# Down's left sums made on VectorE in gate and up, squares a product ahead, and a last stage that starts with the second token half

## The chip, the cores and the metric

The kernel runs on one core of a Trainium2 chip, in one launch. The metric is the device time of one execution in microseconds (us); the times below are of three runs, and the median counts. Times in the trace come from one further, profiled execution.

## The reference, cut to what matters

One layer of a decoder block, batch 1, 1024 tokens, width 1024, all in float32:

```
x1  = x + merge(dilated_attention(n), hgrn2(n))       # n = rmsnorm(x)
h   = silu(rmsnorm(x1) @ w_gate) * (rmsnorm(x1) @ w_up)     # hidden width 2816
x2  = x1 + h @ w_down
g   = sigmoid(rmsnorm(x2) @ w_pg)                     # 1024 x 1024
out = rmsnorm(x2 + g * (p @ w_pe))                    # p: 1024 tokens x 256
```

The change touches the feed-forward part (gate, up, down) and the last stage (w_pg, w_pe, the final norm).

## The kernel before, in words

Activations lie transposed: a tile is 128 channels by 512 or 1024 tokens; `halves` are the token halves c0 and c1 of 512. Each float32 product is three matmuls: an operand is split into a rounded part `hi` (a cast on ACT) and the rest `lo` (a subtraction on DVE), and TensorE adds hi·hi, hi·lo and lo·hi into one PSUM bank (L275, L276, L277 in `product_part`; L192 to L194 in `gemm`).

Gate and up, and then down, use a 2x2 Winograd form: seven block products instead of eight, with sums of blocks as operands. In gate and up the loop over `ft` makes 22 units, each seven products of 12 matmuls. A unit's weights are loaded raw into `w0` and `w1`; four sums s1 to s4 are made from them on POOL (L292 to L295); for each product one left operand `q` is split (L299 on ACT, L300 on DVE). `q` has a ring of five slots, so the splits run up to five products ahead of TensorE. Each unit's result `us` and further sums `t` of it are stored to DRAM, where down finds its right operands (`first_dram`, `second_dram`, `t_dram`).

Down computes products in the order 1, 5, 2, 6, 3, 7, 4. Each has four row tiles d = 0 to 3, and each tile three parts of 4, 4 and 3 blocks: 4 x 33 = 132 matmuls to a product. Per part, `down_lefts` loads one or two raw blocks of w_down into a ring of three slots (256 KB for four blocks, 192 KB for three); products 5, 6, 3 and 7 need a sum on DVE (L1019, L1021, L1023, L1025), and then the split follows (L1027 on ACT, L1028 on DVE) into the same ring of five `q`. Right blocks `B` of the next product are loaded into a staging tile `st` and split (L235 on ACT, L236 on DVE), three after each tile's result (`ahead`). Results are read out of PSUM by `down_result`: copies `m57` on ACT after product 5, and additions and multiplications on DVE after the others. Rows 0 to 3 of x2 are complete (both halves) after product 3, rows 4 to 7 get their second half in product 7 and their first in product 4.

After product 4's tiles, `next_norm` scales x2 by the norm's gain and splits it (L221 on ACT, L222 on DVE) and adds its square to `sums` (L946 on ACT, the addition L947 on POOL). The last stage `ple` then multiplies by w_pg (`weight` splits it: L171 on POOL, L172 on DVE) and by w_pe (p is split by L216 and L217), first half first; a product with ones (L209) adds the squares over the channels.

All DMAs that matter here are issued from SP's queue, which is in order, as is every engine. The order on each engine is decided at build time by a scheduler that follows data, ring slots and the order of the code.

Of the kernel before, what the change touches and what calls it, by code (L numbers as in the profile page):

```python
# [12 lines left out]
F32 = mybir.dt.float32  # L13
# [116 lines left out]
def block_kernel(ctx: ExitStack, tc: tile.TileContext, a: dict, out: bass.AP):  # L130
# [148 lines left out]
    def winograd(units, qr, sr, after=()):  # L279
# [3 lines left out]
        def lefts():  # L283

            for src0, src1, n in units:
# [6 lines left out]
                pool.tensor_add(s1, a21, a22)  # L292
                pool.tensor_sub(s3, a11, a21)
# [65 lines left out]
    act.activation(scratch, eps, AF.Square)  # L359
# [637 lines left out]

    S_SLOTS = [ring([i]) for i in range(16, 22)]

    def down_lefts():  # L1000

        need = {1: ((0, 0),), 5: ((1, 0), (1, 1)), 2: ((0, 1),), 6: ((0, 0),), 3: ((0, 1),), 7: ((0, 0), (1, 0)), 4: ((1, 1),)}
        sums = {}
        for j in DOWN_ORDER:
            for d in range(4):
                for p, (k0, n) in enumerate(PARTS):
                    raw = RAW.next([P, 2, n, P], F32, "w")
                    for i, (row, half) in enumerate(need[j]):
                        nc.sync.dma_start(raw[:, i], a[f"w_dn{p}"][d + 4 * row, half])
                    x, src = raw[:, 0], raw[:, 0]  # L1010
                    if j == 5:
                        if p == 0:
                            sums[d, 0] = S_SLOTS[d].next([P, 2, n, P], F32, "s")
                        if p == 2 and d % 2 == 0:
                            sums[d, 2] = S_SLOTS[4 + d // 2].next([P, 2, n, P], F32, "s")
                    if j in (5, 6, 3):
                        src = sums[d - d % 2, 2][:, d % 2] if p == 2 else sums[d, 0][:, p]
                        if j == 5:
# [14 lines left out]
        [(a["w_gu"][2 * ft], a["w_gu"][2 * ft + 1], 4) for ft in range(NF)], QR, ring([47, 48]), down_lefts()  # L1033
# [17 lines left out]
    rs, down_right = None, {n: [] for n in range(len(DOWN_ORDER))}  # L1051
    for ft in range(NF):
# [19 lines left out]
        us = T.next([P, S], F32, "us")  # L1072
        if ft >= NH:
# [30 lines left out]
    XA, KEEP, OUT = ring([29, 30, 31, 34, 16, 17, 18, 19]), [ring([22, 23]), ring([24, 25])], ring([8, 48])  # L1104
    xa, sums, x3 = {}, pair(SUMS, "sums"), {}
    SQ2 = ring([47])
    X3 = ring(RS[7] + RS[2] + [13, 14, 15, 20, 21, 24, 25, 26])

# [16 lines left out]
    def next_norm(i, c):  # L1125
# [5 lines left out]
        square(i, c, x, sums, SQ2, pool)  # L1131

    def down_result(j, d, b):
# [4 lines left out]
        if j == 2:  # L1138
            t = OUT.next([P, 512], F32, "t")
            x = residual(d)  # L1140
# [4 lines left out]
        if j == 3:  # L1145
            t = OUT.next([P, 512], F32, "t")
# [203 lines left out]
```

## Time and profile before

| | us |
|---|---|
| three runs | 1670.85, 1673.15, 1665.83 (median 1670.85) |
| the profiled execution: time, span of its trace | 1667.34, 1665.5 |
| TensorE busy (x7968 matmuls), mean granted clock | 1604.8, 0.987 |
| VectorE busy | 1117.4 |
| ScalarE busy | 649.5 |
| GpSimd busy | 559.9 |

Busy times are sums over the span and overlap between engines. The engines are called PE (TensorE), DVE (VectorE), ACT (ScalarE), POOL (GpSimd) and SP. PE is busy nearly all the time, so what a change can bring lies in the stretches where it is not; the rows below show them.

### The profile page before, as it was taken

Reading aid. Unit: us, or ns where it says so; the run is one execution under the profiler, and the core shown is the slowest. Engines: PE = TensorE matmul, PEld = TensorE weight load, DVE = VectorE, ACT = ScalarE, POOL = GpSimd, SP = SyncE. Lnnn points to the kernel's source line nnn. Section 1 sums busy time; section 2 is a strip of 40 time slices with the busy share of each in tenths; the row PEclk is TensorE's granted clock in tenths of the full one; section 3 lists DMA queues with packets and bytes.
Section 4 is the critical chain, followed back from the end, with each engine's and each line's share of the span. In section 5 each row is a group of like instructions: output and inputs, shape, how many; then the busy total and the mean of one; then the engine's idle time right before and its main releaser. Section 6 shows DMA issues by size and latency. Waiting matters only on the chain.

```text
span 1665.5 us, 21614 instructions
## 1 busy us (share of the span) xinstructions
PE 1604.8 (96%) x7968; PEld 1332.7 (80%) x7968; DVE 1117.4 (67%) x1673; ACT 649.5 (39%) x1128; POOL 559.9 (34%) x413
## 2 busy tenths in 40 slices
PE   9899998999999999999999999999999999998996
PEld 7687787898998888888887888888888778775786
DVE  8955664678665566765557666666777668798536
ACT  6523332467552011532345333333333554444334
POOL 2555652223322111114354343444554000034214
PEclk9999998999999999999999999999999999999998
DMA  5232343332124322533432323334444887654202
GB/s 197 76 115 102 139 157 116 96 90 72 52 92 146 109 102 77 196 133 114 153 113 83 113 90 99 111 114 140 152 140 163 276 292 232 233 154 128 63 1 101
DMA packets 84778, 213.54 MB, mean 128 GB/s; under 512 B 9408, under 2 KB 16320, under 8 KB 84672
## 3 DMA queue, kind: packets, MB, share of 16 engines
q1 hardware_dynamic: 84528, 212.14, 39.0%
q8 instruction: 62, 1.02, 0.3%
q14 instruction: 44, 0.36, 0.1%
q10 hardware_dynamic: 144, 0.02, 0.0%
HBM read 155.51 MB, written 56.62 MB: 127 GB/s over the span
## 4 chain that ended last, share of the span: by engine, by line
PE 47%; DVE 7%; DMA 4%; issue 2%; ACT 2%; POOL 1%; DVEq 0%; SPq 0%; POOLq 0%; ACTq 0%
PE u L275 8%; PE u L276 8%; PE u L277 8%; PE mm L194 5%; PE mm L192 5%; PE mm L193 5%; DVE B L236 2%; PE g L666 1%; DMA w<-w_dn 1%; DVE q L1028 1%; PE dnb L277 1%; PE dnb L275 1%; PE dnb L276 1%; DMA st<-t_dram 1%; DMA st<-first_dram 1%
## 5 line engine op out<-in xcount | busy, mean ns | idle before, releaser
L275 PE MATMUL u<-B,q 128*128 128x512 f32 x776 | 303.8, 394 | 5.6 <-ACT m L333 3.6
L276 PE MATMUL u<-B,q 128*128 128x512 f32 x776 | 304.4, 392 | 3.7 <-DVE B L236 3.7
L277 PE MATMUL u<-B,q 128*128 128x512 f32 x776 | 303.4, 391 | 1.9 <-DVE q L300 1.9
L275 PEld LDWEIGHTS u<-B,q 128*128 128x128 f32 x776 | 146.6, 189 | 41.5 <-ACT m L333 8.2
L276 PEld LDWEIGHTS u<-B,q 128*128 128x128 f32 x776 | 146.7, 189 | 35.4 <-DVE B L236 5.2
L277 PEld LDWEIGHTS u<-B,q 128*128 128x128 f32 x776 | 146.6, 189 | 32.9 <-DVE q L300 2.3
L299 ACT CAST q<-s 128x512 fp32r<-128x512 f32 x128 | 79.5, 622 | 157.6 <-PE u L277 145.6
L300 DVE TENSOR_TENSOR q<-s,q 128x512 fp32r<-128x512 f32 x128 | 107.5, 842 | 49.2 <-ACT q L299 48.1
L192 PE MATMUL mm<-xh,wh 128*128 128x512 f32 (+1 forms) x352 | 138.1, 392 | 0.1
L194 PE MATMUL mm<-xh,wl 128*128 128x512 f32 (+1 forms) x352 | 132.0, 375 | 1.8 <-DVE wl L172 1.7
L193 PE MATMUL mm<-xl,wh 128*128 128x512 f32 (+1 forms) x352 | 131.4, 373 | 0.0
L171 POOL TENSOR_SCALAR wh<-wr 128x1024 fp32r<-128x1024 f32 (+1 forms) x55 | 57.3, 1044 | 203.9 <-PE mm L193 100.1
L300 DVE TENSOR_TENSOR q<-w,q 128x512 fp32r<-128x512 f32 x96 | 85.0, 886 | 60.2 <-ACT q L299 60.0
L193 PE MATMUL mm<-l,wh 128*128 128x512 f32 (+1 forms) x296 | 115.0, 389 | 1.3 <-DVE l L910 0.9
L192 PE MATMUL mm<-h,wh 128*128 128x512 f32 (+1 forms) x296 | 114.7, 389 | 0.9 <-POOL wh L171 0.8
L194 PE MATMUL mm<-h,wl 128*128 128x512 f32 (+1 forms) x296 | 114.0, 386 | 1.0 <-DVE wl L172 1.0
L299 ACT CAST q<-w 128x512 fp32r<-128x512 f32 x96 | 59.7, 622 | 121.8 <-PE u L277 69.1
L544 POOL TENSOR_SCALAR p<-p,rd 128x128 f32<-128x128 f32 (+3 forms) x64 | 53.1, 831 | 144.3 <-DVE rd L543 126.4
L1082 POOL TENSOR_TENSOR us<-v 128x512 f32<-128x512 f32 x22 | 38.7, 1757 | 155.0 <-DVE v L337 142.2
L194 PEld LDWEIGHTS mm<-xh,wl 128*128 128x128 f32 x352 | 66.3, 188 | 14.5 <-DVE wl L172 3.1
L484 PE MATMUL mm<-wh,xh 128*128 128x256 f32 x256 | 76.4, 300 | 0.0
L485 PE MATMUL mm<-wl,xh 128*128 128x256 f32 x256 | 73.7, 288 | 0.8 <-DVE wl L172 0.8
(303 smaller groups left out, 3847.6 us busy)
## 6 DMA issues: line engine op xcount, KB each, us to landing
w<-w_gu SPq DMA_DIRECT2D x44, 512.0 KB, 3.9
w<-w_dn SPq DMA_DIRECT2D x72, 256.0 KB, 3.9
t_dram<-t SPq DMA_DIRECT2D x44, 256.0 KB, 4.3
w<-w_in SPq DMA_DIRECT2D x20, 512.0 KB, 3.8
st<-t_dram SPq DMA_DIRECT2D x20, 512.0 KB, 4.5
w<-w_dn SPq DMA_DIRECT2D x36, 192.0 KB, 3.8
wr<-w_in SPq DMA_DIRECT2D x13, 512.0 KB, 3.7
sg_dram<-gt SPq DMA_DIRECT2D x24, 256.0 KB, 2.0
```

What stands on the lines that cost most here:

```text
L171: pool.tensor_scalar(hi, raw, 1.0, 0.0, ALU.mult, ALU.add)
L192: pe.matmul(dst, hi[:, k, :], xh[:, c0 : c0 + n], start=first and k == ks[0], stop=False)
L193: pe.matmul(dst, hi[:, k, :], xl[:, c0 : c0 + n], start=False, stop=False)
L194: pe.matmul(dst, lo[:, k, :], xh[:, c0 : c0 + n], start=False, stop=last and k == ks[-1])
L275: pe.matmul(dst, q[:, 0, k], bh, start=first and not more and k == 0, stop=False, skip_group_check=more)
L276: pe.matmul(dst, q[:, 0, k], bl, start=False, stop=False, skip_group_check=more)
L277: pe.matmul(dst, q[:, 1, k], bh, start=False, stop=end, skip_group_check=more)
L299: act.copy(q[:, 0], left[m])
L300: dve.tensor_sub(q[:, 1], left[m], f32(q)[:, 0])
L484: pe.matmul(b, xh[:, ts_], hi[:, k % 4, :], start=(k == 0), stop=False)
L485: pe.matmul(b, xh[:, ts_], lo[:, k % 4, :], start=False, stop=False)
L544: pool.tensor_scalar(pr[:, :n], pr[:, :n], rd, 0.0, ALU.mult, ALU.add)
```

## The change

It has six parts. In gate and up, s1 and s3 are made on DVE (`eng`), s2 and s4 stay on POOL. Twenty-four sums that down's products 5 and 7 need are made in gate and up by `down_sums`: two loads, a sum on DVE (L1010), a store to `left_dram`. Down's products 5 and 7 then load one finished block where they loaded two and added; product 6, which found product 5's sum in SBUF, loads it again and so loads two blocks where it loaded one. The casts of the right blocks are put behind the casts of `q` on ACT (`issue_after`). In down's results, product 7 no longer multiplies `u` and adds it on POOL; product 4 adds `u` first and multiplies after. The squares of rows 0 to 3 are made by product 7, their six additions on POOL; those of rows 4 to 7 are added on DVE. The last stage starts with c1, has the first w_pg weight split during product 4, and finds slots for its weights that are free by then.

```diff
-                pool.tensor_add(s1, a21, a22)
-                pool.tensor_sub(s3, a11, a21)
+                eng.tensor_add(s1, a21, a22)
+                eng.tensor_sub(s3, a11, a21)
...
+    left_dram = {j: [dr.tile([4, P, n, P], F32, name=f"s{j}_{p}_dram") for p, (_, n) in enumerate(PARTS)] for j in (5, 7)}
+    LS = ring([28, 32])
+
+    def down_sums():
+        for d in range(4):
+            for p, (_, n) in enumerate(PARTS):
+                for j in (5, 7):
+                    raw = LS.next([P, 2, n, P], F32, "ls")
+                    other = (d + 4, 1) if j == 5 else (d, 0)
+                    nc.sync.dma_start(raw[:, 0], a[f"w_dn{p}"][other])
+                    nc.sync.dma_start(raw[:, 1], a[f"w_dn{p}"][d + 4, 0])
+                    (dve.tensor_add if j == 5 else dve.tensor_sub)(raw[:, 0], raw[:, 0], raw[:, 1])
+                    nc.sync.dma_start(left_dram[j][p][d], raw[:, 0])
+                    yield
...
-                    for i, (row, half) in enumerate(need[j]):
-                        nc.sync.dma_start(raw[:, i], a[f"w_dn{p}"][d + 4 * row, half])
+                    if j in need:
+                        row, half = need[j]
+                        nc.sync.dma_start(x, a[f"w_dn{p}"][d + 4 * row, half])
+                    else:
+                        nc.sync.dma_start(x, left_dram[j][p][d])
+                    if j == 6:
+
+                        nc.sync.dma_start(raw[:, 1], left_dram[5][p][d])
...
-                        if j == 5:
-                            dve.tensor_add(src, x, raw[:, 1])
-                        elif j == 6:
-                            dve.tensor_sub(src, src, x)
+                        if j == 6:
+                            dve.tensor_sub(src, raw[:, 1], x)
...
-                    if j == 7:
-                        dve.tensor_sub(src, x, raw[:, 1])
...
+        if 0 < ft < NF - 2:
+            for _ in islice(to_sum, 1 + (ft % 3 == 0)):
+                pass
...
-        square(i, c, x, sums, SQ2, pool)
+
+    def add_square(i, c, eng):
+        x = xa[i][:, halves[c]]
+        if i == 0:
+            act.activation(sums[c], x, AF.Square)
+        else:
+            turn["sq"] += 1
+            sq = squares[:, turn["sq"] % 2]
+            act.activation(sq, x, AF.Square)
+            eng.tensor_add(sums[c], sums[c], sq)
...
-            dve.tensor_mul(u[d], u[d], rs[0])
-            pool.tensor_add(x[:, c0], x[:, c0], u[d])
         if j == 4:
-            t, x = OUT.next([P, 512], F32, "t"), xa[d + 4]
-            dve.tensor_mul(t, b, rs[0])
+            t, x = temp(), xa[d + 4]
+            dve.tensor_add(t, b, u[d])
+            dve.tensor_mul(t, t, rs[0])
             dve.tensor_add(x[:, c0], x[:, c0], t)
...
-            for _ in islice(ahead, 3):
-                pass
-
+
+            with tc.issue_after(latest(act_engine)):
+                for _ in islice(ahead, 3):
+                    pass
+
+            if j == 7:
+                for c in range(2):
+                    add_square(d, c, pool)
             if j == 4:
-                for c in range(2):
-                    next_norm(d, c)
+                if d == 1:
+                    w_pg0 = weight(a["w_pg"][0], [P, KD, P], WH, WL)
+                next_norm(d, 1)
                 next_norm(d + 4, 1)
+                add_square(d + 4, 1, dve)
+                next_norm(d, 0)
     for d in range(4):
         next_norm(d + 4, 0)
+        add_square(d + 4, 0, dve)
...
     for d in range(4):
-        w = weight(a["w_pg"][d], [P, KD, P], WH, WL)
-        for cs in halves:
+        w = weight(a["w_pg"][d], [P, KD, P], WH, WL) if d else w_pg0
+        for cs in halves[::-1]:
             ple(d, w, cs.start, 512)
```

On DVE, in an early unit of gate and up, before (L300 is the `lo` of a left, L335 and L337 and L1063 read PSUM):

```order
L1089 TENSOR_TENSOR t1_1007_7710<-us_1006_7702 128x512
L300 TENSOR_TENSOR q_1015_7751<-s12_994_7615,q_1015_7751 128x512
L335 TENSOR_TENSOR v_1012_7718<-u_1010_7716,m_1011_7717 128x512
L300 TENSOR_TENSOR q_1020_7777<-w0_1016_7767,q_1020_7777 128x512
L1063 TENSOR_TENSOR gs_1021_7792<-u_1008_7714,rs_1000_7682 128x512
L300 TENSOR_TENSOR q_1022_7795<-s12_1018_7771,q_1022_7795 128x512
L300 TENSOR_TENSOR q_1023_7810<-s34_1019_7772,q_1023_7810 128x512
L300 TENSOR_TENSOR q_1024_7825<-w0_1016_7767,q_1024_7825 128x512
L337 TENSOR_TENSOR v_1012_7718<-u_1009_7715,m_1011_7717 128x512
```

and the same place after (L1010 is a sum for down, `ls` its two-slot tile):

```order
L1010 TENSOR_TENSOR ls_1089_8287<-ls_1089_8287 128x384
L300 TENSOR_TENSOR q_1015_7757<-s12_994_7621,q_1015_7757 128x512
L1010 TENSOR_TENSOR ls_1109_8431<-ls_1109_8431 128x384
L292 TENSOR_TENSOR s12_1018_7777<-w1_1017_7774 128x512
L335 TENSOR_TENSOR v_1012_7724<-u_1010_7722,m_1011_7723 128x512
L300 TENSOR_TENSOR q_1020_7783<-w0_1016_7773,q_1020_7783 128x512
L1081 TENSOR_TENSOR gs_1021_7798<-u_1008_7720,rs_1000_7688 128x512
L300 TENSOR_TENSOR q_1022_7801<-s12_1018_7777,q_1022_7801 128x512
L300 TENSOR_TENSOR q_1023_7816<-s34_1019_7778,q_1023_7816 128x512
L1010 TENSOR_TENSOR ls_1130_8576<-ls_1130_8576 128x512
L1010 TENSOR_TENSOR ls_1131_8581<-ls_1131_8581 128x512
L300 TENSOR_TENSOR q_1024_7831<-w0_1016_7773,q_1024_7831 128x512
```

Two pairs of the sums stand in this unit's row, and so in each of the first six units that have any: the code asks for one or two a unit, the scheduler brings them forward. The sum s1 (L292) stands between them.

On ACT, at the end of product 5, before (`q_1535` is product 2's first left, `B` the right blocks, `m57` the copy that frees a bank):

```order
L1027 CAST q_1533_11199<-s_1521_11130 128x384
L235 CAST B_1537_11231<-st_1536_11229 128x512
L235 CAST B_1538_11234<-st_1536_11229 128x512
L1027 CAST q_1535_11216<-w_1534_11214 128x512
L235 CAST B_1540_11239<-st_1539_11237 128x512
L235 CAST B_1547_11291<-st_1539_11237 128x512
L1137 COPY m57_1461_10779<-dnsp1505_11036 128x512
```

and after:

```order
L1044 CAST q_1551_11280<-w_1550_11278 128x512
L1044 CAST q_1553_11297<-w_1552_11295 128x384
L1044 CAST q_1555_11314<-w_1554_11312 128x512
L1173 COPY m57_1487_10907<-dnsp1528_11153 128x512
L235 CAST B_1557_11329<-st_1556_11327 128x512
L235 CAST B_1558_11332<-st_1556_11327 128x512
```

No right block stands any more between product 5's last left and product 2's first, nor directly ahead of the copy `m57`.

On PE, behind the last matmul of down, before (`sums` with ones, then p with w_pe, with w_pg's c0 half further on):

```order
L277 MATMUL dnov1684_12089<-B_1733_12376,q_1763_12534 128x512
L209 MATMUL mm_1807_12723<-sums_1457_10775,ones_70 128x512
L192 MATMUL mm_1808_12730<-h_1785_12657,wh_1791_12669 128x512
L192 MATMUL mm_1811_12769<-h_1785_12657,wh_1791_12669 128x512
L193 MATMUL mm_1808_12730<-l_1786_12658,wh_1791_12669 128x512
L193 MATMUL mm_1811_12769<-l_1786_12658,wh_1791_12669 128x512
L194 MATMUL mm_1808_12730<-h_1785_12657,wl_1792_12670 128x512
L194 MATMUL mm_1811_12769<-h_1785_12657,wl_1792_12670 128x512
L209 MATMUL mm_1806_12716<-sums_1456_10774,ones_70 128x512
```

and after:

```order
L277 MATMUL dnov1702_12189<-B_1747_12458,q_1774_12616 128x512
L209 MATMUL mm_1799_12771<-sums_1481_10901,ones_70 128x512
L192 MATMUL mm_1797_12745<-xh_1754_12516,wh_1765_12581 128x512
L193 MATMUL mm_1797_12745<-xl_1755_12517,wh_1765_12581 128x512
L194 MATMUL mm_1797_12745<-xh_1754_12516,wl_1766_12582 128x512
L192 MATMUL mm_1797_12745<-xh_1767_12585,wh_1765_12581 128x512
```

What follows down's last matmul is now a whole product of 24 matmuls of c1 with w_pg's first tile, whose operands are all split before down ends; the six of p with w_pe and the second ones-product come behind it. The bank of that product is the one that down's last tile (`dnov`) leaves.

## Rows read from the trace of the kernel before

**Rows 1.** The page's busy time, share of the span and instructions by engine.

```profile
PE 1604.8 (96%) x7968; PEld 1332.7 (80%) x7968; DVE 1117.4 (67%) x1673; ACT 649.5 (39%) x1128; POOL 559.9 (34%) x413
```

**Rows 2.** Windows of 25 us: PE, PEld, DVE, ACT, POOL busy (x instructions), granted clock, DMA share, GB/s.

```profile
1350.00:1375.00 25.00, 22.07 (x88) 17.22 (x88) 15.71 (x26) 14.00 (x26) 0.00 (x0) 0.93 0.84 283
...
1450.00:1475.00 25.00, 24.24 (x106) 19.23 (x105) 20.67 (x34) 12.54 (x22) 2.04 (x2) 1.00 0.77 240
1475.00:1500.00 25.00, 23.20 (x99) 17.93 (x97) 24.94 (x28) 13.58 (x24) 13.61 (x9) 1.00 0.31 86
1500.00:1525.00 25.00, 20.81 (x89) 16.27 (x89) 23.80 (x30) 8.65 (x17) 10.12 (x6) 1.00 0.37 103
1525.00:1550.00 25.00, 20.33 (x71) 13.00 (x70) 18.41 (x18) 9.69 (x12) 10.48 (x8) 0.93 0.52 166
1550.00:1575.00 25.00, 25.00 (x112) 20.71 (x111) 12.69 (x18) 9.83 (x15) 5.75 (x5) 1.00 0.14 43
```

**Rows 3.** Timeline of PE where product 5 ends: start, us, line [idle before <- releaser].

```profile
1355.04 0.39 PE L277 MATMUL dnsp<-B,q 128*128 128x512 f32 x1
1357.35 0.50 PE L275 MATMUL dnb<-B,q 128*128 128x512 f32 x1 [1.92 <-ACT q L1027]
...
1359.82 0.80 PE L275 MATMUL dnsp<-B,q 128*128 128x512 f32 x1 [0.84 <-ACT m L1137]
```

**Rows 4.** Timeline of ACT in the same place.

```profile
1355.64 1.14 ACT L235 CAST B<-st 128x512 fp32r<-128x512 f32 x2 [0.96 <-DMA st<-second_dram]
1356.68 0.61 ACT L1027 CAST q<-w 128x512 fp32r<-128x512 f32 x1
```

**Rows 5.** Windows of product 5 and of product 6.

```profile
1325.00:1357.00 32.00, 30.43 (x135) 24.86 (x133) 23.77 (x41) 16.80 (x32) 0.00 (x0) 1.00 0.91 302
...
1390.00:1421.00 31.00, 31.00 (x138) 25.66 (x138) 27.09 (x47) 13.35 (x24) 0.00 (x0) 1.00 0.73 233
```

**Rows 6.** Groups of instructions from 1450 to 1530 us: busy, mean ns | idle before.

```profile
L947 POOL TENSOR_TENSOR sums<-sums,sq 128x512 f32<-128x512 f32 x13 | 20.3, 1559 | 18.3 <-ACT sq L946 18.3
...
L1157 POOL TENSOR_TENSOR xa<-xa,u 128x512 f32<-128x512 f32 x4 | 7.0, 1738 | 169.0 <-DVE u L1156 159.8 <-issue 6.2 <-PE dnov L277 3.0
...
L1156 DVE TENSOR_TENSOR u<-u,rs 128x512 f32<-128x512 f32 x4 | 2.7, 681 | 0.0
...
L1025 DVE TENSOR_TENSOR w<-w 128x384 f32<-128x384 f32 x3 | 1.6, 550 | 1.0 <-DMA w<-w_dn 1.0
```

**Rows 7.** Timeline of DVE in product 7, and a row of product 4.

```profile
1477.21 0.68 DVE L1025 TENSOR_TENSOR w<-w 128x512 f32<-128x512 f32 x1
...
1478.41 1.77 DVE L236 TENSOR_TENSOR B<-st,B 128x512 fp32r<-128x512 f32 x1
...
1505.51 0.74 DVE L222 SCALAR_TENSOR_TENSOR xl<-xa,vec,xh 128x512 fp32r<-128x512 f32 x1
```

**Rows 8.** Timeline of PE where the last stage begins.

```profile
1528.62 0.73 PE L192 MATMUL mm<-h,wh 128*128 128x512 f32 x2 [0.39 <-POOL wh L171]
1529.69 0.73 PE L193 MATMUL mm<-l,wh 128*128 128x512 f32 x2 [0.34 <-DVE l L217]
1531.43 0.73 PE L194 MATMUL mm<-h,wl 128*128 128x512 f32 x2 [1.01 <-DVE wl L172]
1533.21 1.49 PE L209 MATMUL mm<-sums,ones 128*128 128x512 f32 x2 [1.05 <-POOL sums L947]
```

**Rows 9.** Timeline of DVE there: down's last result and a weight's `lo`.

```profile
1527.41 0.69 DVE L1160 TENSOR_TENSOR t<-dnov,rs 128x512 f32<-128x512 f32 x1 [1.00 <-PE dnov L277]
...
1530.16 1.21 DVE L172 TENSOR_TENSOR wl<-wr,wh 128x1024 fp32r<-128x1024 f32 x1
```

**Rows 10.** Ten units of gate and up (905 to 1095 us), groups of instructions.

```profile
L1083 DVE TENSOR_TENSOR us<-us,gs 128x512 f32<-128x512 f32 x10 | 17.9, 1786 | 0.0
L293 POOL TENSOR_TENSOR s<-w,w 128x512 f32<-128x512 f32 x10 | 17.8, 1776 | 0.5 <-DMA w<-w_gu 0.2
```

**Rows 11.** One line of gate and up by itself: durations, first and last start.

```profile
L1082 POOL TENSOR_TENSOR us<-v x11: 1799/1803/1807, 900.2 to 1090.6; 128x512 f32<-128x512 f32 x11
```

**Rows 12.** A window in gate and up.

```profile
900.00:925.00 25.00, 25.00 (x112) 20.57 (x111) 18.79 (x26) 9.39 (x17) 11.00 (x7) 1.00 0.39 119
```

**Rows 13.** DMA issues of the whole span: KB each, median us to landing.

```profile
w<-w_dn SPq DMA_DIRECT2D x72, 256.0 KB, 3.9
t_dram<-t SPq DMA_DIRECT2D x44, 256.0 KB, 4.3
```

More of the change, by code (lines that the diff above doesn't have):

```diff
@@ L277, in product_part, with winograd @@
             pe.matmul(dst, q[:, 1, k], bh, start=False, stop=end, skip_group_check=more)
-    def winograd(units, qr, sr, after=()):
+    def winograd(units, qr, sr, after=(), eng=pool):
         def lefts():
@@ L358, in block_kernel @@
     scratch = cp.tile([P, 1], F32, name="scratch")
-    act.activation(scratch, eps, AF.Square)
+    act_engine = act.activation(scratch, eps, AF.Square).ins.engine
     warm = MS.next([P, 512], F32, "warm")
@@ L1032, in block_kernel @@
     ffn_unit, next_left, _ = winograd(
-        [(a["w_gu"][2 * ft], a["w_gu"][2 * ft + 1], 4) for ft in range(NF)], QR, ring([47, 48]), down_lefts()
+        [(a["w_gu"][2 * ft], a["w_gu"][2 * ft + 1], 4) for ft in range(NF)], QR, ring([47, 48]), down_lefts(), dve
     )
@@ L1051, in block_kernel @@
     rs, down_right = None, {n: [] for n in range(len(DOWN_ORDER))}
+    to_sum = down_sums()
     for ft in range(NF):
@@ L1100, in block_kernel, with temp @@
             nc.sync.dma_start(t_dram[7][i], t23[:, 1])
-    XA, KEEP, OUT = ring([29, 30, 31, 34, 16, 17, 18, 19]), [ring([22, 23]), ring([24, 25])], ring([8, 48])
+    XA, KEEP, OUT = ring([29, 30, 31, 34, 16, 17, 18, 19]), [ring([22, 23]), ring([24, 25])], ring([8])
     xa, sums, x3 = {}, pair(SUMS, "sums"), {}
-    SQ2 = ring([47])
     X3 = ring(RS[7] + RS[2] + [13, 14, 15, 20, 21, 24, 25, 26])
+    temps, squares = OUT.next([P, 2, 512], F32, "t"), ring([47]).next([P, 2, 512], F32, "sq")
+    turn = {"t": 0, "sq": 0}
+    def temp():
+        turn["t"] += 1
+        return temps[:, turn["t"] % 2]
     def bank_set(n):
@@ L1138, in down_result @@
         if j == 2:
-            t = OUT.next([P, 512], F32, "t")
-            x = residual(d)
+            t, x = temp(), residual(d)
             dve.tensor_mul(t, b, rs[0])
@@ L1145, in down_result @@
         if j == 3:
-            t = OUT.next([P, 512], F32, "t")
+            t = temp()
             dve.tensor_add(t, b, u[d])
@@ L1150, in down_result @@
         if j == 7:
-            t, x = OUT.next([P, 512], F32, "t"), residual(d + 4)
+            t, x = temp(), residual(d + 4)
             dve.tensor_add(m57[d], b, m57[d])
@@ L1194, in block_kernel @@
     wpe = [weight(a["w_pe"][j], [P, 2, 512], PW, PW) for j in range(2)]
-    rs = None
+    rs = {}
     sumf, rf = RF.next([P, S], F32, "sumf"), RF.next([P, S], F32, "rf")
     def ple(d, w, c0, n):
-        nonlocal rs
-        cs = slice(c0, c0 + n)
+        cs, c = slice(c0, c0 + n), c0 // 512
         b = mm()[:, :n]
         gemm(b, w, x3, c0, n, range(KD))
-        if rs is None:
-            rs = pair(RS2, "rs3")
-            token_scale(rs, sums, [T4.next([P, 512], F32, "t") for _ in range(2)])
+        if c not in rs:
+            rs[c] = RS2.next([P, 512], F32, "rs3")
+            rstd_rep(rs[c], sums[c], mm(), 1.0 / D, *(T4.next([P, 512], F32, "t") for _ in range(2)))
         hi, lo = wpe[d // 4]
@@ L1211, in ple @@
         t = T4.next([P, 512], F32, "t")[:, :n]
-        dve.tensor_mul(t, b, rs[c0 // 512][:, c0 % 512 : c0 % 512 + n])
+        dve.tensor_mul(t, b, rs[c][:, c0 % 512 : c0 % 512 + n])
         act.activation(t, t, AF.Sigmoid)
```

17 lines of the change are left out of this document (8 added, 9 removed).

## The prediction

> **What bounds the kernel now.** I read the page's busy times first. PE is busy for 96% of the span [rows 1], so only idle or slow PE time can be won, and the question is where it lies. The windows of 25 us answer that. At its full rate PE does 112 matmuls in 25 us, 0.223 us each (the last of [rows 2]); every matmul that a window lacks is 0.223 us lost, whether PE waited or ran at a lower clock. The window from 1350 lacks 24 matmuls (5.4 us), that from 1450 lacks 6 (1.3), from 1475 13 (2.9), from 1500 23 (5.1) and from 1525 41, which is 9.2, of which I count 1.1 as the slower products with ones and keep 8.1. Together 22.8 us in five windows, all in down and at the change to the last stage. Gate and up show full windows like [rows 12]: nothing can be won there, only lost.
>
> Then the timelines, for each of these places. Where product 5 ends, PE waits 1.92 us for a left and 0.84 us for the copy `m57` [rows 3]. On ACT that left stood behind two casts of right blocks, and those had waited for their transfer [rows 4]: the cause is a late DMA, passed on by ACT's order. The window holds a clock of 0.93 as well [rows 2], between the two levels of 1.2 and 2.4 GHz, after PE had idled; so the loss of 5.4 us is larger than the waits. In product 5 the DMA engines were busy 0.91 of the time at 302 GB/s, in product 6 0.73 at 233 [rows 5]. From 1475 to 1525 the DMA share is only 0.31 and 0.37, but DVE is busy 24.94 and 23.80 of 25 us [rows 2]: DVE is the bound of products 7 and 4. Part of that is not its own work. The same kind of addition takes 0.68 us when alone and 1.77 us when POOL works beside it [rows 7], and POOL has 15 instructions in these 50 us [rows 2]. At the change to the last stage PE waits in turn for `wh`, `l`, `wl` and POOL's last `sums` [rows 8], which are all made only when down has ended.
>
> **The change, part by part.**
>
> Product 5. Twelve parts now load one block instead of two: 8 x 256 KB and 4 x 192 KB, 2.8 MB less of the 9.7 MB that 302 GB/s moved in 32 us, so about 215 GB/s, below what product 6 moves today without a wait [rows 5]. The twelve sums leave DVE, and ACT has the left and the copy ahead of the right blocks. Either alone should remove the waits of [rows 3]. Of 5.4 us I leave 0.5: **-4.9** (bounds 0 and -5.4).
>
> Product 6. It loads what product 5 saved: 7.2 + 2.8 MB in 31 us, 323 GB/s, more than product 5's 302. That is a rate at which the kernel stalled, but here with product 2's lighter stretch ahead of it, in which the three raw slots and five lefts fill, and with the lefts first on ACT. Bounds 0 and +5.4 (product 5's loss again); nearer the lower because of that lead: **+2.0**.
>
> Products 7 and 4. Of DVE's 48.7 us in the 50 from 1475, three `u` multiplications (0.68 each) and two or so sums of product 7's lefts (0.55 to 0.68 [rows 6, 7]) go: 3.2 us. All of POOL's additions go too (L947 1.56 us each, L1157 1.74 [rows 6]; rows 0 to 3 have their six additions earlier). They stretched DVE's work by up to 15 x 1.09 = 16.4 us; I take 13, because POOL's additions did not always meet a DVE instruction of that kind. Added are seven additions of squares, three additions of `u` (0.68 each) and one `wl` of 1.21 us [rows 9]: 8.0. Demand after: 48.7 - 3.2 - 13 + 8.0 = 40.5 us. PE's work in these 50 us is 50 - 8.0 = 42 us. So DVE would still be busy for 96% of it, which is bare cover: the queue is in order, and its instructions come in bunches behind each result. Of the 8.0 us lost I leave 3.0: **-5.0** (bounds 0, if the 13 were only 11 and bunching ate the rest, and -8.0). The 1.3 us of the window from 1450 stay.
>
> The Trainium skill (SBUF — State Buffer, section "Who interferes with whom") says that a VectorE instruction with two inputs in SBUF and a GpSimd instruction that reads SBUF exclude each other, the later one being blocked fully. The trace agrees: 0.68 and 1.77 us in [rows 7]. Taken to the letter, the whole 16.4 us would go and the term would be the full -8.0.
>
> The change to the last stage. Of the 8.1 us, the waits in [rows 8] make 2.8, the rest is low clock behind them and waits further on. Afterwards PE has 24 matmuls of c1 at once (5.4 us), whose operands and whose `wl` exist before down ends, and `l` and the second `sums` are wanted behind these. What is late next is the bank: the first product takes the one that down's last tile leaves, and DVE reads it about 1.0 us after the last matmul and for 0.69 us [rows 9], with one or two instructions of 1.2 us ahead of it in its row. So I leave 3.0: **-5.1** (bounds -2 and -8.1).
>
> Gate and up. s1 and s3 come to DVE (2 x 0.68) where POOL took 1.78 us for s3 [rows 10]. In six units four sums are added (4 x 0.68): 4.1 us in a unit of 19.04 us (190.4 us over ten, [rows 11]). DVE was busy 18.79 of 25 us there, 14.3 in a unit [rows 12], hence 18.4 of 19.04 at worst: it still fits, with five lefts of lead as cover. If that cover goes, each microsecond over is lost. At the very first unit the sum s3 stands before right blocks on DVE. I take **+1.1** for both (bounds 0 and the first rival).
>
> Nothing in the reordering of the token halves changes the number of matmuls.
>
> Sum: -4.9 + 2.0 - 5.0 - 5.1 + 1.1 = -11.9 us against the profiled execution's 1667.3, so 1655.4. The median of the runs shown, 1670.85, lies 3.5 above that execution and the fastest 1.5 below it; I add half of 3.5 and forecast **1657 us**.
>
> **The rivals.**
>
> First, and on the other side: the round trip of down's sums blocks DVE. A pair of sums needs its loads (3.9 us), two additions (1.4) and stores (4.3) [rows 13] before the two slots are free: 9.6 us, and a unit has two such pairs, 19.2 us of a unit of 19.04. The additions stand in DVE's row ahead of lefts and results, so a late load stops all that PE needs. For six units at 9.6 us that is 1 us behind, covered by four products of lead (4 x 2.7 = 10.9 us). At 12 us a round (every transfer 1.3 times its median, since SP also issues the unit's weights and waits for each sum before its store) it is (24 - 19.04) x 6 - 10.9 = 19 us lost: 1676. It cancels the gain from 11.4 us a round on. Against it: the DMA share is 0.39 there [rows 12], so the transfers have room. Chance 0.06.
>
> Second: the stretch bound by DMA only moves from product 5 to 6, with the whole 5.4 us: 3.4 more than forecast, 1660.5. For it speaks the 323 GB/s, against it the lead. Chance 0.18.
>
> Third: moving additions from POOL to DVE gains nothing, as DVE does then what it waited for before. A stretched instruction loses 1.09 us, an addition takes 0.68 itself; were these even, the 3.2 us removed would only balance three additions of `u` (2.0) and the `wl` (1.2), and of the lost 8.0 some 2 would return, for the three squares' additions that come before these 50 us: 3.0 more than forecast, 1660. Chance 0.17. The Trainium skill (Perfetto Trace Analysis, section "Optimizing Scalar/DVE Operations") has this rule: the two engines share a read port, so offloading between them might not help. By it the time would be this 1660; the rows speak half against it, since 1.09 is more than 0.68.
>
> Fourth: all of the 22.8 us vanishes, since the clock recovers when the waits in front of it go: 1644.5 + 1.7 = 1646. Chance 0.12.
>
> Fifth: the casts and slots do nothing, because each place has another wait directly behind the first: around 1668, no change. Chance 0.06.
>
> **How the numbers follow.** My case has 0.41, the others as given. A measurement of this kernel can tell about 0.5%, 8.4 us, from no change; so faster means below 1662.5. The forecast, the second and the third case lie 5.5, 2 and 2.5 us below that, the fourth far below. I take 0.88 of the first, 0.7 of the second, 0.75 of the third and all of the fourth: 0.36 + 0.13 + 0.13 + 0.12 = 0.74. The first rival gives 0.05 of slower, and 0.21 is left for no change. The range from 1646 to 1665 leaves out the first and fifth rival and little of the rest.
>
> **What would show it.** Right: the windows around product 5's end full; no wait of PE for `q` in products 7 and 4 beyond 3 us, with POOL almost idle and DVE's lefts at 0.68; behind down's last matmul one wait of 1 to 3 us for the bank instead of four; units of gate and up still 19.04 us apart. Wrong: a DMA share near 0.95 in product 6 and waits for `q` or `B` at its end (second rival); DVE still at 24 of 25 us in products 7 and 4 (third); L1010 waiting for `ls` in the first seven units and units longer than 19.04 us (first). The prediction falls most easily at the size of the term for products 7 and 4, where the demand on DVE comes within 2 us of what there is time for.

## The result and the profile after

The changed kernel took 1648.88 us (median of four runs, 1643.22 to 1653.13) where the kernel before took 1672.0 in the runs beside it: a ratio of 0.9869 (95% interval 0.9845 to 0.9893), which is some 22 us less. Run again beside other kernels it gave 1647.31 us and 0.9868 (0.9852 to 0.9885). I had forecast 1657 from 1670.85, so 14 us less: the direction and the range hold, the gain is half as large again as forecast.

The page's busy times after, as in [rows 1]:

```profile
PE 1599.5 (97%) x7968; PEld 1334.9 (81%) x7968; DVE 1119.2 (68%) x1725; ACT 651.9 (39%) x1130; POOL 475.7 (29%) x357
```

PE has the same 7968 matmuls; DVE has 52 instructions more and hardly more busy time, POOL 84 us less. The windows of 25 us, as in [rows 2]:

```profile
1350.00:1375.00 25.00, 25.00 (x112) 20.52 (x111) 12.35 (x20) 12.50 (x24) 0.00 (x0) 1.00 0.63 197
...
1425.00:1450.00 25.00, 23.82 (x106) 19.38 (x104) 19.57 (x34) 10.99 (x21) 0.56 (x1) 1.00 0.83 258
1450.00:1475.00 25.00, 24.42 (x99) 19.47 (x100) 17.99 (x30) 13.18 (x25) 3.30 (x3) 0.93 0.58 186
1475.00:1500.00 25.00, 25.00 (x112) 20.71 (x111) 25.00 (x42) 16.73 (x29) 0.00 (x0) 1.00 0.51 153
1500.00:1525.00 25.00, 24.96 (x108) 20.03 (x108) 23.45 (x32) 9.12 (x13) 7.54 (x5) 1.00 0.59 181
1525.00:1550.00 25.00, 25.00 (x110) 20.36 (x109) 18.49 (x24) 14.12 (x20) 5.91 (x5) 1.00 0.30 91
```

The end of product 5 is full, product 4 is full, the change to the last stage is full but for the products with ones. DVE is busy for the whole of 1475 to 1500 us and yet PE misses nothing. Only 1425 to 1475, around product 3's end, has lost more than before: 19 matmuls are missing there, where 6 were missing before (the window from 1425 had its 112). These are all the waits of PE in down and the last stage, as total us, number of waits and the longest:

```profile
PE mm L1285 <- POOL sumf L1273: 2.3, 1, 2.3
PE dnb L275 <- ACT q L1044: 1.7, 1, 1.7
PE mm L209 <- DVE t L1269: 1.3, 1, 1.3
PE dnb L275 <- ACT B L235: 0.9, 2, 0.6
PE dnb L276 <- DVE B L236: 0.2, 1, 0.2
```

To compare traces I take stages from first matmul to first matmul, in us; a full product is 29.92, and products 5 and 2, and 3 and 7, stand together because their tiles interleave at the border. The left column is the time from the last ones-product of the attention and hgrn2 part to down's first matmul. It holds the product with w_out, 157.1 to 157.2 us in every trace, and then gate and up.

```
                    gate,up  p1     p5+2   p6     p3+7   p4     last    span
before              584.17   33.26  65.15  29.92  61.32  37.99  138.29  1665.5
before_again        583.91   33.10  64.48  29.92  66.02  37.26  139.81  1669.1
after               585.71   32.33  59.96  29.92  63.86  29.93  131.29  1651.3
after_again         586.00   32.98  59.96  29.92  62.00  29.93  129.91  1646.4
no_sums             585.44   32.78  64.52  29.92  62.09  29.93  135.32  1654.2
squares_pool        586.04   33.42  59.96  29.92  62.16  29.93  137.97  1657.7
c0_first            585.85   31.98  59.96  29.92  61.70  29.92  134.87  1651.0
squares_old         586.95   32.88  59.97  29.92  59.98  34.11  135.79  1654.3
no_issue_after      585.40   32.15  62.19  29.92  67.99  29.93  131.52  1657.4
s13_pool            587.31   32.68  59.97  29.92  61.29  29.93  131.50  1648.7
squares_behind      587.28   33.38  59.98  29.92  61.72  30.22  138.90  1656.6
squares_pool_bank   587.75   31.97  59.95  29.92  61.94  29.92  132.25  1650.5
sq_u_old            586.30   32.98  59.96  29.92  60.13  37.36  139.75  1661.0
pin_bank            586.68   32.76  59.98  29.92  59.98  29.92  131.16  1644.2
```

The mean of two traces after less the mean of two before: gate and up +1.8, product 1 -0.5, products 5 and 2 -4.9, 3 and 7 -0.7, product 4 -7.7, last stage -8.5. Together -20.5 us, about the measured 22. The stages ahead of the left column, the same in both programs, ended 2.9 us later in the changed kernel's first trace and 0.3 us later in its second: chance, and the reason why the first pair of spans differs by only 14.2 us. Single stages differ between two traces of one kernel as well: the last stage of the changed kernel by 1.4 us, all of it in its last 35 us, and products 3 and 7 of the kernel before by 4.7 us. A difference of 1 to 2 us in one trace is therefore no finding by itself.

### The profile page after: what moved, and what is told of

It reads as the page before. It is cut to its first block, busy times and chain, and to the rows that moved or that the text cites. A ratio compares the mean times of both kernels' runs of the same rounds, so it can differ in the third digit from the quotient of the medians.

```text
span 1651.3 us, 21727 instructions
## 1 busy us (share of the span) xinstructions
PE 1599.5 (97%) x7968; PEld 1334.9 (81%) x7968; DVE 1119.2 (68%) x1725; ACT 651.9 (39%) x1130; POOL 475.7 (29%) x357
## 3 DMA queue, kind: packets, MB, share of 16 engines
q8 instruction: 62, 1.02, 0.3%
## 4 chain that ended last, share of the span: by engine, by line
PE 47%; DVE 6%; DMA 5%; issue 2%; POOL 1%; ACT 1%; SPq 0%; DVEq 0%; POOLq 0%
PE u L275 7%; PE u L276 7%; PE u L277 7%; PE mm L192 5%; PE mm L194 5%; PE mm L193 5%; PE dnb L275 2%; PE dnb L277 2%; PE dnb L276 2%; DVE B L236 1%; DMA s_dram<-ls 1%; PE g L666 1%; DMA ls<-w_dn 1%; DMA w<-s_dram 1%; DMA w<-w_dn 1%
## 5 line engine op out<-in xcount | busy, mean ns | idle before, releaser
L277 PEld LDWEIGHTS u<-B,q 128*128 128x128 f32 x776 | 146.7, 189 | 34.1 <-DVE q L300 3.3
L300 DVE TENSOR_TENSOR q<-s,q 128x512 fp32r<-128x512 f32 x128 | 107.3, 841 | 40.9 <-ACT q L299 40.1
L194 PE MATMUL mm<-xh,wl 128*128 128x512 f32 (+1 forms) x352 | 132.3, 376 | 0.1
L300 DVE TENSOR_TENSOR q<-w,q 128x512 fp32r<-128x512 f32 x96 | 91.9, 958 | 51.1 <-ACT q L299 51.0
L294 POOL TENSOR_TENSOR s<-s,w 128x512 f32<-128x512 f32 x32 | 45.1, 1410 | 107.4 <-DVE s L292 88.2
```

Of the source, the lines that this page charges most:

```text
L194: pe.matmul(dst, lo[:, k, :], xh[:, c0 : c0 + n], start=False, stop=last and k == ks[-1])
L277: pe.matmul(dst, q[:, 1, k], bh, start=False, stop=end, skip_group_check=more)
L294: pool.tensor_sub(s2, s1, a11)
L300: dve.tensor_sub(q[:, 1], left[m], f32(q)[:, 0])
```

## The experiments

Ten edits of the changed kernel, and both kernels once more. A ratio is to the kernel before in the runs beside it.

**The changed kernel again** (no edit).

> The changed kernel once more, nothing altered. It is the base of the three that run beside it, and its trace tells what of the difference between the two profiled executions (14.2 us of span) repeats. Up to the end of the stage before gate and up the two programs are the same, and yet the changed one's trace stood 2.9 us later there (first matmul with ones of that stage's last group); by my reading that is chance, and this run should show from -2 to +3 us there, 16 to 20 us less than before in all. The rival, that the change itself delays the start, would show the same +2.9 again.

1647.31 us, ratio 0.9868; the late start did not repeat, 19.1 us of span less than before.

**Without the sums made in gate and up.**

```diff
-        if 0 < ft < NF - 2:
-            for _ in islice(to_sum, 1 + (ft % 3 == 0)):
-                pass
...
-                    else:
-                        nc.sync.dma_start(x, left_dram[j][p][d])
...
+                    for i, (row, half) in enumerate(need[j]):
+                        nc.sync.dma_start(raw[:, i], a[f"w_dn{p}"][d + 4 * row, half])
...
+                        if j == 5:
+                            dve.tensor_add(src, x, raw[:, 1])
...
+                    if j == 7:
+                        dve.tensor_sub(src, x, raw[:, 1])
```

> The changed kernel without the sums made in gate and up: products 5 and 7 load two blocks and add on DVE as before, product 6 finds product 5's sum in SBUF. If the second load was what made product 5 late, the loss at its end (5.4 us before, none after) comes back with a DMA share of about 0.9 in product 5, products 7 and 4 lose 1 to 3 us to the twelve sums, and gate and up win about 1.3: 5 to 8 us slower than the changed kernel. If ACT's order alone (casts of the left ahead of the right blocks) had cured product 5, its end stays full and the kernel is within 2 us of the changed one, or faster.

1654.68 us, 0.9914 (0.9899 to 0.9929): 7.4 us slower than the changed kernel beside it. Products 5 and 2 take 64.5 us again, so the second load, with the addition on DVE that goes with it, was the cause of most of their loss, with ACT's better order in place; the run does not tell the load from the addition. Product 4 stays full without the sums made earlier. The rest is lost at the last stage, 5.4 us against the second trace of the changed kernel; 3.7 of them lie at its start, where PE waits 2.1 us for DVE to read down's last bank.

**ACT's order alone undone.**

```diff
-            with tc.issue_after(latest(act_engine)):
-                for _ in islice(ahead, 3):
-                    pass
+            for _ in islice(ahead, 3):
+                pass
```

> The changed kernel without the rule that puts the casts of right blocks behind those of lefts on ACT. Products 5 and 2 lost 5.3 us before, 4.7 with the second loads put back, 0.1 with both changes. If the lighter DMA load alone cured them, they stay within 1 us of full and the kernel within 1 us of the changed one. If both are needed, 2 to 5 us come back there.

0.9934 (0.9920 to 0.9948), against 0.9868. My reading, that lighter load alone cures product 5, falls: 2.2 us come back there. Products 3 and 7 take 4 to 6 us more than in the changed kernel; this is one trace, and there the kernel before differs from itself by 4.7 us. These are the two waits in this run's timeline of PE:

```profile
1360.24 0.50 PE L275 MATMUL dnb<-B,q 128*128 128x512 f32 x1 [1.78 <-ACT q L1044]
...
1455.75 0.79 PE L275 MATMUL dnb<-B,q 128*128 128x512 f32 x1 [5.19 <-ACT q L1044]
```

**The eight additions of squares on POOL again.**

```diff
-                add_square(d + 4, 1, dve)
+                add_square(d + 4, 1, pool)
...
-        add_square(d + 4, 0, dve)
+        add_square(d + 4, 0, pool)
```

> The changed kernel with the eight additions of the squares of rows 4 to 7 on POOL again; rows 0 to 3 stay where the change put them. If POOL's additions stretch DVE's (1.77 instead of 0.68 us), eight of them cost DVE up to 8.7 us and spare it 5.4; in products 7 and 4 DVE is busy for 49 of 51 us, so PE loses 2 to 5 us there. If moving between the two engines is neutral, the time is that of the changed kernel within 1 us, and DVE's busy time in these windows is the same.

1654.03 us, 0.9917 (0.9901 to 0.9932): 6.7 us slower, but not where I had put it. Product 4 stays at 29.93; the last stage takes 138.0. First the timeline of PE behind down's last matmul, then that of DVE, then that of POOL:

```profile
1519.73 1.02 PE L209 MATMUL mm<-sums,ones 128*128 128x512 f32 x2
1524.87 0.76 PE L192 MATMUL mm<-xh,wh 128*128 128x512 f32 x1 [4.12 <-DVE t L1193]
```

```profile
1521.85 2.28 DVE L172 TENSOR_TENSOR wl<-wr,wh 128x1024 fp32r<-128x1024 f32 x1
1524.05 0.68 DVE L1193 TENSOR_TENSOR t<-dnov,u 128x512 f32<-128x512 f32 x1
```

```profile
1520.14 1.25 POOL L171 TENSOR_SCALAR wh<-wr 128x1024 fp32r<-128x1024 f32 x1 [4.39 <-DMA wr<-w_pe]
1521.36 1.69 POOL L1167 TENSOR_TENSOR sums<-sums,sq 128x512 f32<-128x512 f32 x1
```

PE wants the bank `dnov`; DVE reads it only after a `wl` of w_pe that stands ahead in its row, and that `wl` needs a `wh` whose weight landed at 1520, and then takes 2.28 us beside POOL's addition instead of 1.21. The load of that weight was issued 3.3 us ahead of down's last matmul here and 9.1 us ahead of it in the changed kernel. There the same place reads, on DVE and then on PE:

```profile
1519.11 1.21 DVE L172 TENSOR_TENSOR wl<-wr,wh 128x1024 fp32r<-128x1024 f32 x1
1520.24 0.68 DVE L1193 TENSOR_TENSOR t<-dnov,u 128x512 f32<-128x512 f32 x1
```

```profile
1520.01 1.02 PE L209 MATMUL mm<-sums,ones 128*128 128x512 f32 x2
1521.07 0.47 PE L192 MATMUL mm<-xh,wh 128*128 128x512 f32 x1
```

The `wl` is done just in time: DVE starts to read the bank 0.2 us after PE went on to the ones-product and ends at 1520.92, 0.15 us before PE takes the bank.

**The same with another bank for the last stage's first product.**

```diff
     x3 = [x3[i] for i in range(KD)]
+    mm()
```

> The kernel with eight additions on POOL again, but the first product of the last stage takes another PSUM bank than the one that down's last tile leaves (one bank of the ring is passed over). In that kernel PE waited 4.1 us for DVE to read down's last tile, with product 4 itself at its full 29.9 us, and the last stage took 138.0 us instead of 129.9 to 131.3. If that bank is the price of DVE's backlog, the wait is gone here and the last stage takes about 131 us: some 6 us faster than with POOL alone, near the changed kernel. If DVE's backlog is paid in any case, the wait only moves (to the weight, to sums or to the next operand), and the time stays.

0.9889 (0.9875 to 0.9904): the last stage falls from 138.0 to 132.3 us. So the bank was the larger part of the price; what is left are waits of 1.3 us for an `xl` and 0.4 us for `sums`, some 15 us after down's end.

**All squares where they were, on POOL.**

```diff
-            if j == 7:
-                for c in range(2):
-                    add_square(d, c, pool)
...
+                for c in (1, 0):
+                    next_norm(d, c)
+                    add_square(d, c, pool)
+                    if c:
+                        next_norm(d + 4, 1)
+                        add_square(d + 4, 1, pool)
...
+        add_square(d + 4, 0, pool)
```

> The changed kernel with all squares where they were before: those of rows 0 to 3 made in product 4 too, all 14 additions on POOL. If it is POOL's additions among DVE's work that filled DVE in product 4, product 4 loses again, 3 to 8 us of its 8.1, and the bank that the last stage needs first comes late on top (4.1 us with eight additions on POOL): 8 to 13 us slower than the changed kernel. If the twelve sums and the products of u were what filled it, product 4 stays at its full 29.9 us, and the time is within 2 us of the kernel that had only the eight additions on POOL.

0.9961 (0.9948 to 0.9974). Product 4 takes 34.1 us, so half of its loss comes back, with a wait for a left of 2.3 us; behind it PE waits 4.5 us for the bank. In the kernel with eight additions on POOL product 4 was full. The two differ only in the squares of rows 0 to 3: it is their six additions that cost product 4 its 4.2 us, and the eight moved to DVE gave it nothing. Products 3 and 7 are full here, 59.98 us. I read this as a price of the squares made a product ahead; the end of product 3, below, shows otherwise.

**The squares and the products of u as before.**

```diff
             dve.tensor_add(x[:, c1], x[:, c1], t)
+            dve.tensor_mul(u[d], u[d], rs[0])
+            pool.tensor_add(x[:, c0], x[:, c0], u[d])
         if j == 4:
             t, x = temp(), xa[d + 4]
-            dve.tensor_add(t, b, u[d])
-            dve.tensor_mul(t, t, rs[0])
+            dve.tensor_mul(t, b, rs[0])
```

> All squares as before and the products of u as before too (the multiplication in product 7, the addition on POOL), so that of all that eased DVE in products 7 and 4 only the twelve sums made earlier are left. With the squares alone undone product 4 took 34.1 us; before it took 38.0, full is 29.9. If the four additions on POOL are the other half, product 4 takes 36 to 38 us; if the sums' absence is, it stays at about 34.

0.9987 (0.9974 to 0.9999). Product 4 takes 37.4 us, as in the kernel before (37.3 and 38.0), although the twelve sums are still made earlier. So POOL's 14 + 4 additions among DVE's work, with the four multiplications on DVE that belong to them, bring all of its loss back; the sums have no share that these traces can tell.

**The squares of rows 0 to 3 behind the casts on ACT.**

```diff
-                for c in range(2):
-                    add_square(d, c, pool)
+                with tc.issue_after(latest(act_engine)):
+                    for c in range(2):
+                        add_square(d, c, pool)
```

> The changed kernel with the squares of rows 0 to 3 put behind the casts on ACT. Where product 3 ends the changed kernel lost 2.2 and 4.0 us in two traces, and product 7's first left stood on ACT behind a square and a norm that waited for a result of product 3. If that order makes the loss, it wins 1.5 to 2.5 us there, and products 3 and 7 take about 60 us together instead of 62 to 63.9. If the late loads of product 7's lefts make it, nothing changes there.

0.9934 (0.9920 to 0.9948): no better where product 3 ends (61.7 us), and worse at the last stage (138.9), where the bank came 5.8 us late. POOL's additions for these rows ran from 1473 to 1492 us, beside DVE in product 7, where the changed kernel had those of c0 from 1385 to 1402 and those of c1 from 1449 to 1467; DVE read the last bank 6 us after down's end. That the one led to the other is argued, not shown.

**The c1 squares behind product 7's first lefts, and another bank.**

```diff
+        if j == 7:
+            pin = latest(act_engine)
         for d in range(4):
...
-                for c in range(2):
-                    add_square(d, c, pool)
+                add_square(d, 0, pool)
+                with tc.issue_after(pin):
+                    add_square(d, 1, pool)
...
     x3 = [x3[i] for i in range(KD)]
+    mm()
```

> An attempt at a faster one: the changed kernel with the c1 squares of rows 0 to 3 put behind the first lefts of product 7 on ACT (those of c0 stay early), and with another bank for the last stage's first product. If the squares made the loss of 2.2 to 4.0 us where product 3 ends, products 3 and 7 take 59.9 to 60.5 us together, the last stage about 130, and the kernel is 1.5 to 4 us faster than the changed one. If the later squares only move DVE's and POOL's work into product 4, that one takes more than 29.9 us and the gain is nothing.

1646.96 us, 0.9868 (0.9853 to 0.9883). From product 5 on every product of down is full, and these are PE's waits from down's start to the end:

```profile
PE mm L1288 <- POOL sumf L1276: 2.3, 1, 2.3
PE dnb L275 <- ACT B L235: 1.4, 2, 0.8
PE mm L209 <- DVE t L1272: 1.3, 1, 1.3
PE dnb L276 <- DVE B L236: 0.2, 1, 0.2
```

I expected this if the squares made the loss at product 3's end; that they did is not shown, as told below. The 2 to 4 us do not show in the ratio, which is that of the changed kernel within its interval; the trace alone has the gain.

**The first half first in the last stage.**

```diff
-        for cs in halves[::-1]:
+        for cs in halves:
```

> The changed kernel with the last stage's four row tiles taken first half first again; the first w_pg weight is still split during product 4. If what counts is that c1's operands are split before down ends, then c0, whose last rows are made by the last product, waits for them: 3 to 7 us slower, with PE waits behind down's last matmul for xh, xl or sums. If only the early weight counted, it is within 1 us of the changed kernel.

1654.23 us, 0.9914 (0.9899 to 0.9930): 6.9 us slower than the changed kernel beside it, 5.0 us of it in the last stage's trace, 4.6 at its start, with waits of 1.5 us for `xh` and 0.9 us for `xl`. The operands count, not the early weight alone.

**s1 and s3 on POOL.**

```diff
-        [(a["w_gu"][2 * ft], a["w_gu"][2 * ft + 1], 4) for ft in range(NF)], QR, ring([47, 48]), down_lefts(), dve
+        [(a["w_gu"][2 * ft], a["w_gu"][2 * ft + 1], 4) for ft in range(NF)], QR, ring([47, 48]), down_lefts()
```

> The changed kernel with s1 and s3 of gate and up on POOL as before. From the end of the earlier stage to down the kernel before took 584.2 us, the changed one 585.7 to 586.0, without down's sums 585.4: so s1 and s3 on DVE should cost 1.3 us, in the first unit, and this run wins about that and has 584.5 to 585. If the two sums on DVE relieve something later in gate and up (POOL beside DVE in every unit), it is not faster: 586 or more.

0.9888 (0.9874 to 0.9902), gate and up 587.3 us: not faster. That DVE's s1 and s3 cost the 1.3 us was wrong: the first unit takes 26.2 us here, as in the changed kernel's first trace, and the second and fourth take 20.0 and 21.4 us, where the changed kernel has 19.1 to 19.2 and 20.4 to 20.9.

**The kernel before again**, one execution.

> The kernel before once more, nothing altered, for a second trace of it. Its products of down should repeat to a tenth of a microsecond where PE was full, and if the losses at product 5's end, in product 4 and at the last stage are the program's and not chance, they repeat within 1 us each (65.2 us for products 5 and 2, 38.0 for product 4, 138.3 for the last stage). Gate and up took 584.2 us in the first trace and 585.4 to 587.8 in eight traces with the change or parts of it: if the change costs 1 to 2 us there, this run has 584 to 585 again; if the first trace was merely quick, it has 586.

Products 5 and 2 64.5, product 4 37.3, the last stage 139.8: the program's losses repeat. Gate and up 583.9 again. What varies is the end of product 3, 61.3 and 66.0 us, where PE waited 3.3 us for a left this time.

## Why the prediction was right in kind and short in size

Every place named gave back what it had lost, and the three remainders that I had left for product 6, for product 4 and for the last stage (2.0, 3.0 and 3.0 us) were not there.

**Product 5** (-4.9 forecast, -4.9 measured). The size is right; the reason was half right. I wrote that either alone, the lighter load or ACT's order, would remove the waits. Neither does: with the order alone 4.6 of the 4.9 us are lost, with the lighter load alone 2.2. That the term came out to a tenth is luck: it rests on both.

**Product 6** (+2.0 forecast, 0). It moved more, as computed, and without a wait:

```profile
1390.00:1421.00 31.00, 31.00 (x138) 25.67 (x137) 23.10 (x40) 14.06 (x26) 3.91 (x2) 1.00 0.83 275
```

That is 275 GB/s, not the 323 of my sum. The loads of product 6 stand earlier than that window: its twelve pairs are issued from 1381 to 1408 us, and from 1381 to 1412 the DMA engines moved 287 GB/s at a share of 0.87, with 139 matmuls of PE. That the lead in the slots is what let PE go on is argued, not shown. The second rival falls.

**Products 7 and 4** (-5.0 forecast; measured -7.7 in product 4). The mechanism held: POOL's additions stretched DVE's, and with the squares and then the products of u back on POOL the loss comes back in two halves. The 13 us of stretching that I took were about right. An estimate from the traces, from DVE's instructions that start between 1475 and 1525 us and the quickest one of the same line and shape: together they took 13.1 and 15.3 us longer than that in the two traces before, 2.8 and 3.7 us in the two after. The remainder of 3.0 us for bunching was wrong, and so was the demand of 40.5 us: DVE is busy 48.45 of these 50 us, 25.00 of the first 25, with 74 instructions where it had 58, and PE still waits for nothing from 1475 to the end of down. That the five lefts of lead absorb the order in which DVE does its work is how I read it. That DVE is full does not say that it is late. And the sums taken off DVE there, which I counted at 1.2 of the 3.2 us removed, did nothing for product 4.

The third rival was that moving additions from POOL to DVE gains nothing. Its time, 1660, falls, but for product 4 it was half right. Eight of them put back left product 4 full. What relieved it were the squares of rows 0 to 3 made a product ahead, with their six additions still on POOL (4.2 us), and the products of u (3.3 us). The eight cost 6.7 us all the same, most of it through the bank behind down's end. The Trainium skill (Perfetto Trace Analysis, section "Optimizing Scalar/DVE Operations") says that offloading between these two engines might not help because they share a port; product 4 agrees with it, 29.93 us either way, and the last stage does not, 129.9 to 131.3 against 138.0. An addition on DVE takes 0.68 us; on POOL these took 1.3 to 2.3 us.

**The change to the last stage** (-5.1 forecast, -8.5 measured). The step that failed is the remainder of 3.0 us for the bank. The bank is indeed what comes next, and in four of the experiments PE waited 2.1 to 5.8 us for it; but in the changed kernel the ones-product of 1.02 us covers the read, with some 0.15 us to spare in both traces. The forecast named the place and not how near it is to a wait: that it cost nothing is luck. When the `wl` of w_pe was late, the stage took 5.4 to 9.0 us longer than in the changed kernel's second trace.

**The end of product 3** was not in my sum, beyond the 1.3 us that were to stay. In the changed kernel a square and a norm (`xh`) of rows 0 to 3 stand on ACT ahead of product 7's first left and wait for product 3's results. ACT, and PE behind it:

```profile
1448.73 0.63 ACT L1166 ACTIVATE sq<-xa 128x512 f32<-128x512 f32 x1 [2.71 <-DVE xa L1184]
1449.27 0.71 ACT L221 ACTIVATE xh<-xa,vec 128x512 fp32r<-128x512 f32 x1
1449.88 0.60 ACT L1044 CAST q<-w 128x512 fp32r<-128x512 f32 x1
```

```profile
1450.54 0.50 PE L275 MATMUL dnb<-B,q 128*128 128x512 f32 x1 [1.72 <-ACT q L1044]
```

It cost 2.2 and 4.0 us. I took the squares for the cause, and the traces speak against it. With all squares on POOL, where products 3 and 7 are full, ACT has the same square and the same norm ahead of the same left:

```profile
1443.77 0.63 ACT L1166 ACTIVATE sq<-xa 128x512 f32<-128x512 f32 x1 [0.91 <-DVE xa L1184]
1444.30 0.71 ACT L221 ACTIVATE xh<-xa,vec 128x512 fp32r<-128x512 f32 x1
1445.02 0.62 ACT L1044 CAST q<-w 128x512 fp32r<-128x512 f32 x1
```

And with the squares of these rows behind the casts no square stands there, and 1.9 us are lost. What goes with the loss is a load. Earlier in product 3 DVE waits for a block of w_down, first in the changed kernel, then with all squares on POOL:

```profile
1436.85 0.69 DVE L1042 TENSOR_TENSOR s<-w,s 128x512 f32<-128x512 f32 x1 [2.93 <-DMA w<-w_dn]
```

```profile
1431.88 0.69 DVE L1042 TENSOR_TENSOR s<-w,s 128x512 f32<-128x512 f32 x1 [2.24 <-DMA w<-w_dn]
```

Counted from product 3's first matmul that wait ended after 10.6 and 7.5 us. In the three traces with full products 3 and 7 it ended after 7.5 to 7.7 us. In the other seven that have both the earlier sums and ACT's order it ended after 8.8 to 10.6 us, and the loss grows with it, from 1.5 to 4.0 us. DVE's later work, product 3's results among it, shifts along. All ten issue these loads in the same order. Why some land later, and whether chance put the three without loss together, stays open.

Whether ACT's order gave something back there rests on one trace (8.2 us lost without it, against 1.5 and 6.2 in the kernel before).

**Gate and up** (+1.1 forecast, +1.8 measured). The first rival's place is real and its price small. DVE waited for down's blocks in ten places, and PE once:

```profile
DVE ls L1010 <- DMA ls<-w_dn: 15.4, 10, 3.2
```

```profile
952.39 0.50 PE L275 MATMUL u<-B,q 128*128 128x512 f32 x1 [1.26 <-DVE v L335]
```

The five lefts of lead covered the rest, as the forecast said. By the first matmuls of its 22 units, everything behind the first unit took 400.8 and 400.6 us before, 402.4 and 402.0 after and 400.6 without the sums: 1.5 us are theirs, nearly all in the fourth unit, where PE's wait stands (19.1 us before, 20.9 and 20.4 after). So the units did not all stay 19.04 us apart, as I had asked for. The remaining 0.3 us lie in the first unit. It took 26.2 and 26.1 us before, 26.2 and 26.8 after, and 26.1 to 27.8 over all traces, with no edit that it follows: what is left there looks like chance.

One reading of mine was too quick: gate and up are not full everywhere. The window from 875 to 900 us of the kernel before has 85 matmuls, in the first unit, and that from 1300 to 1325, in product 1, has 97. Neither was in my 22.8 us, and the change left both nearly as they were (product 1 -0.5 us).

The fourth rival, that all 22.8 us vanish, was nearest: 1646 against 1648.88. I had given it 0.12 because I took each remainder singly as likely. Two of the three, for product 4 and for the bank, were not independent: both hung on DVE's row being far enough ahead, and it was, at the bank by little. The rival is not wholly right either, since product 3's end still lost 2.2 and 4.0 us.

## What to carry to other kernels

An engine that is busy all the time in a stretch can still be early: look at whether its results are waited for, not at its busy share, before leaving a remainder. When a wait stands behind work that a change has moved, look for a run in which the work stands in the same place and the wait does not: the square ahead of product 7's first left looked like the cause of a loss, and with the same square in the same place another kernel lost nothing. At a change of stage ask which PSUM bank the next product takes, what stands ahead of the instruction that frees it, and by how much it is in time.

## What the hardware showed beyond that

A wait of PE can cost more than its length, where the granted clock falls behind it. In the kernel with eight additions on POOL, PE idled for 4.1 us behind down's last matmul:

```profile
1520.00:1525.00 5.00, 0.88 (x3) 0.16 (x1) 4.72 (x4) 0.00 (x0) 4.57 (x3) 0.82 0.66 210
1525.00:1530.00 5.00, 5.00 (x12) 3.94 (x13) 4.94 (x4) 1.97 (x2) 4.00 (x3) 0.50 0.75 220
1530.00:1535.00 5.00, 5.00 (x23) 4.10 (x23) 5.00 (x5) 3.10 (x4) 3.36 (x2) 1.00 0.60 202
```

For the next five microseconds the clock was 0.50, the lower of its two levels of 1.2 and 2.4 GHz, with 12 matmuls where 22 to 24 fit, and then full again: 6.5 us lost here against the second trace of the changed kernel, for 4.1 us of waiting. (The other 1.6 of the stage's 8.1 us lie in the last 35 us, where the two traces of the changed kernel differ by 1.4.) The three other waits for this bank, of 2.1, 4.5 and 5.8 us, cost 3.7, 5.9 and 7.6 us there.

The traces also bear out how far DVE and POOL exclude each other: the same `wl` took 1.21 us alone and 2.28 us beside an addition of POOL that took 1.69. The Trainium skill (SBUF — State Buffer, section "Who interferes with whom") has the second of the two blocked until the first is done. POOL's addition had 1.20 us to go when the `wl` began, and the `wl` was 1.07 us longer, so the trace agrees.
